# Queries and keys of a diffusion layer, computed with channels on partitions and read back in four parts

## The chip, the core and the metric

The kernel runs on one core of a Trainium2 chip. The metric is the time of one execution in microseconds (us) of the device; the profile's span leaves out a little at its ends. The engines are TensorE (PE in the profile, with its weight loads as PEld), VectorE (DVE), ScalarE (ACT), GpSimd (POOL) and SyncE (SP), which issues most transfers.

## What is computed

One layer of a diffusion backbone: 1024 latent tokens of 1024 channels and 256 context tokens are normalised and modulated, run through differential attention and a bidirectional state-space mixer side by side, merged, and then through a mixture of 64 experts. The part that the change touches is the first projection, the rotary embedding of queries and keys, and what the attention reads of them:

```python
q, k, v, z, xbc, dt_raw, gates = jnp.split(h @ w_in, IN_SPLITS, axis=-1)
...
q = apply_rope(q.reshape(nb, ns, N_ATTN_HEADS, 2, ATTN_DH), cos, sin)
k = apply_rope(k.reshape(nb, ns, N_ATTN_HEADS, 2, ATTN_DH), cos, sin)
...
kc = (hc @ w_k).reshape(nb, nl, N_ATTN_HEADS, 2, ATTN_DH)
...
k_all = jnp.concatenate([kc, k], axis=1)
...
def apply_rope(u, cos, sin):
    half = ATTN_DH // 2
    uf = u.astype(jnp.float32)
    rot = jnp.concatenate([-uf[..., half:], uf[..., :half]], axis=-1)
    return (uf * cos[:, None, None, :] + rot * sin[:, None, None, :]).astype(u.dtype)
```

There are 8 heads of two halves (c = 0, 1), each half with 64 channels of q and k. Context tokens have keys but no rotation and no queries.

## The kernel before

The kernel goes through its stages one behind the other, each one's end mixed with the next one's start: normalisation and q, k, v (0 to 391 us), the state-space mixer (to about 1040), attention (to about 1500), the branches and their merge (to about 1640), the experts (to the end).

**What sets the order.** The instructions are emitted by a planner at build time, the class `Flow`. Each piece of work is a Python generator, a stream with a priority, that yields what it needs next (a tile, a free buffer of a ring, an engine). The planner has a clock of its own for each engine and costs for each operation (a GpSimd transfer is put at 1050 ns of that engine), and always goes on with the stream that can start first; at a tie, the higher priority. So a change of one stream's operations can move the instructions of all others, and every engine then runs its own queue strictly in that order.

**Precision.** Every product is made in three matmuls (`mm3`, L420): numbers are split in a high and a low part (`hi`, `lo` for weights, `hh`, `hl` for h), and high x high, high x low and low x high are summed in a PSUM bank. The split is a cast by ScalarE (`F.acopy`, L165) and a subtraction by VectorE (`F.tt`, L172). `F.ptt` (L176) is the GpSimd form.

**q, k and v (`norm_and_qkv`, L492).** Six blocks of 512 columns of the weights, k, v, q, k, v, q, with 8 chunks of 128 channels each. `weights` loads and splits a block's weights, `modulate` makes h of the three groups of tokens (g = 0: the 256 of the context; g = 1, 2: 512 latent tokens each; h lies with channels on partitions) from transposes of x. `main` runs over tiles of 128 tokens: the tile's h is the stationary side, 512 columns of weights stream, and 24 matmuls fill one bank of the ring `acc` (4 banks). In the first block, the first three tiles are done in two halves of the channels (k 0 to 3, then 4 to 7). The adaLN vectors (`wa`, `cw`, `adab`, `wacc`) are worked out meanwhile.

**After a tile (`post_qk`, L662).** The bank has 128 tokens on partitions. VectorE multiplies it with the rope table (one product `ra` of 512 columns, two `rb` of 256), GpSimd adds the two into `r` (L176; for context tokens ScalarE copies instead), TensorE transposes `r` in four pieces into a bank of `tr` (L153), ScalarE casts this to the high part `sa`, VectorE subtracts for the low part `sb`. Two tiles share an `sa` and an `sb`; when both are full, SyncE stores them to DRAM (`s.qk`) in parts of 64 partitions.

**The seam.** `mixer_t` (L791) starts with dt: matmuls with 64 columns of weights, a fold (`aux<-fold,G`), then ScalarE and VectorE work out dt (`dtn`), which TensorE reads as `aux<-dtn,cst`. The convolution's matmuls (`acc<-hh,hi` with 128 columns) come beside these.

**Attention.** A tile `qk` of 128 partitions x 3328 numbers holds all that a head's half needs: for q its high and low part, for k its high and low part, so 1.70 MB. `attention_ahead` (L1326) loads them with `swdma` (L225), issued from GpSimd's queue, into a ring of three buffers: one transfer for each (h, c), when a buffer comes free. The scores are the matmuls `sps<-qk`; `e` is VectorE's and ScalarE's softmax, `tr<-cst,e` transposes it and `pv<-wr,vv` is the product with v. `branches` (L1196) gives matmuls of the merge (`bacc`, three for each product) as work of lower priority that fills gaps of TensorE in the planner's clock.

Of the kernel before, what the change touches and what calls it, by code (L numbers as in the profile page):

```python
# [9 lines left out]
F32 = mybir.dt.float32  # L10
F32R = mybir.dt.float32r
# [3 lines left out]
ALU = mybir.AluOpType  # L15
# [4 lines left out]
P = 128  # L20
D = 1024
KC = 8
T = 1024
# [26 lines left out]
def host_consts():  # L50
    j = np.arange(P)
    eye = np.eye(P, dtype=np.float32)
    le = (j[:, None] <= j[None, :]).astype(np.float32)
    ge = (j[:, None] >= j[None, :]).astype(np.float32)
    ones = np.ones((P, P), np.float32)
    cst = np.concatenate([eye, le, ge, ones], axis=1)
    row = np.repeat(np.arange(T // 64, dtype=np.float32), 64)
    col = np.tile(np.arange(64, dtype=np.float32), T // 64)
    inv = np.float32(10000.0) ** (-np.arange(0, 32, 2, dtype=np.float32) / np.float32(32))
    inv = inv.astype(np.float32)  # L60
    ang = np.concatenate([row[:, None] * inv, col[:, None] * inv], axis=-1)
    cos, sin = np.cos(ang), np.sin(ang)
    rope = np.concatenate([cos, cos, -sin, sin], axis=-1).astype(np.float32)
# [313 lines left out]
class Layer:  # L377
# [114 lines left out]
    def norm_and_qkv(s):  # L492
# [28 lines left out]
        st = {"wa": [], "x": 0, "w": 0, "normed": 0, "mod": 0, "done": [set(), set(), set()], "cols": 0, "blocks": 0, "ada": False, "q": None, "two": {}}  # L521
# [114 lines left out]

        def weights():
            for n, (kind, j) in enumerate(blocks):
                c0 = {"q": COL_Q, "k": COL_K, "v": COL_V}[kind] + j * 512
                for a in (0, 4):  # L640
# [8 lines left out]
                    yield from s.splits([(hi[:, b:b + 2], lo[:, b:b + 2], raw[:, b:b + 2]) for b in (0, 2)],  # L649
# [12 lines left out]
        def post_qk(ps, kind, j, t):  # L662
            yield [lambda: st["q"] is not None]
            rr, ras, rbs, sas, sbs, rope = (st["q"][n] for n in ("r", "ra", "rb", "sa", "sb", "rope"))
            if t < 2:
                yield [ps, rr, "ACT"]
                r = rr.get()
                F.acopy(r, ps.rearrange("p (h x) -> p h x", x=64))
                acc.put(ps)
            else:  # L670
                yield [ps, rope, ras, rbs, "DVE"]
                cs = rope[:, t - 2, :]
                pv = ps.rearrange("p (h x) -> p h x", x=64)
                ra, rb = ras.get(), rbs.get()
# [3 lines left out]
                acc.put(ps)  # L678
                yield [ra, rb, rr, "POOL"]
                r = rr.get()  # L680
                F.ptt(r, ra, rb, ALU.add)
                ras.put(ra)
                rbs.put(rb)
            yield [r, tr]
# [3 lines left out]
            two = st["two"].setdefault((kind, j, t // 2), [])  # L688
            yield [pt, "ACT"] + ([] if two else [sas, sbs])
            if not two:  # L690
                two += [sas.get(), sbs.get(), 0]
            a, b = two[:2]
            (av, bv), pv = (w.rearrange("p (m h c) -> h p m c", m=4, h=2)[t % 2] for w in (a, b)), pt.rearrange("p (m c) -> p m c", m=4)
            F.acopy(av, pv)
            yield [a, "DVE"]
            F.tt(bv, pv, av.bitcast(F32), ALU.subtract)
            tr.put(pt)
            two[2] += 1
            if two[2] == 2:
                o0 = (t // 2 - (kind == "q")) * 2 * P  # L700
                dst = s.qk[j].rearrange("(m u) (v x) c -> v u x m c", u=2, v=2)
                for w, v, o in ((a, 0, 0), (a, 1, 0), (b, 0, T), (b, 1, T)) if kind == "q" else ((a, 0, 2 * T), (b, 1, 2 * T)):
                    for u in range(2):
                        F.dma(dst[v, u][:, :, o + o0:o + o0 + 2 * P], w[64 * u:64 * u + 64].bitcast(F32).rearrange("x (m c) -> x m c", m=4))
                sas.put(a)
                sbs.put(b)
            rr.put(r)

        def main():
            for n, (kind, j) in enumerate(blocks):  # L710
                tiles = list(range(2 if kind == "q" else 0, 10))
                steps = [(t, 0, KC) for t in tiles]
                if n == 0:
                    steps = [(t, a, a + 4) for a in (0, 4) for t in tiles[:NH]] + steps[NH:]
                banks = {}
                for t, k0, k1 in steps:
                    yield [lambda: len(ready) >= 2 * n + k1 // 4]
                    tok = slice(t * P, (t + 1) * P)
                    g = 0 if t < 2 else 1 if t < 6 else 2
                    sl = slice((t - spans[g][0]) * P, (t - spans[g][0] + 1) * P)  # L720
                    hh, hl = s.h[g]
                    yield [lambda: st["done"][g].issuperset(range(k0, k1))] + ([] if k0 else [acc])
                    ps = banks.pop(t) if k0 else acc.get()
                    for k in range(k0, k1):
                        wh, wl = ready[2 * n + k // 4]
                        if k % 4 == 0:
                            yield [wh, wl, hh, hl]
                        s.mm3(ps, hh[:, k, sl], hl[:, k, sl], wh[:, k % 4], wl[:, k % 4], k == 0, k == KC - 1)
                    if k1 < KC:
                        banks[t] = ps  # L730
                    else:
                        F.spawn(1, post_v(ps, j, tok) if kind == "v" else post_qk(ps, kind, j, t))
                ws = ready[2 * n:2 * n + 2]
                his, los = sets[n % 2]
                for hi, lo in ws:
# [14 lines left out]
        st["q"] = q = {"r": s.ring(qp, [P, 8, 64], "r", 2), "ra": s.ring(qp, [P, 8, 64], "ra", 2),  # L750
                       "rb": s.ring(qp, [P, 8, 64], "rb", 2), "sa": s.ring(qp, [P, 1024], "sa", 2, F32R),
                       "sb": s.ring(qp, [P, 1024], "sb", 2, F32R), "rope": qp.tile([P, 8, P], F32, name="rope")}
        F.dma(q["rope"], I["rope"].rearrange("(t p) c -> p t c", p=P))
# [572 lines left out]
    def attention_ahead(s, go):  # L1326

        F = s.F
# [1172 lines left out]
```

## Time and profile before

| | |
|---|---|
| timed runs, median (lowest to highest) | 2770.72 us (2765.67 to 2773.66), 3 runs |
| the profiled execution | 2762.38 us, span 2760.1 us |
| TensorE busy | 2610.2 us, 95% of the span |
| VectorE, ScalarE, GpSimd busy | 73%, 49%, 33% |
| granted TensorE clock, mean | 0.979 |

The profile is of one execution. In the timeline the end of a matmul is modelled and runs over into the next one, so what a matmul costs is read from the distance of two starts, not from its duration. [...] Idle time before an instruction stands in brackets with what ended it.

### The profile page before, as it was taken

The numbers are of one execution on the slowest core, as the hardware profiler recorded it, in microseconds if no ns is written. First come the engines' busy times: TensorE is split into PE (matmuls) and PEld (weight loads), VectorE is DVE, ScalarE is ACT, GpSimd is POOL, SyncE is SP. The second block draws the span as 40 slices with busy tenths as digits, with TensorE's granted clock in tenths as the row PEclk, the third lists the DMA queues.
The fourth block names the chain that finished last, engine by engine and source line by source line (L and its number), as shares of the span: only waits on it lengthen the run. The fifth ranks groups of instructions, "written<-read, shape, count | busy, mean of one in ns | idle before, by whom it ended". The sixth has DMA issues, their size and how long they took to land.

```text
span 2760.1 us, 41127 instructions
## 1 busy us (share of the span) xinstructions
PE 2610.2 (95%) x14561; PEld 2099.0 (76%) x14561; DVE 2012.4 (73%) x4680; ACT 1341.9 (49%) x2104; POOL 920.9 (33%) x669
## 2 busy tenths in 40 slices
PE   7999999999999998999999999899999999999992
PEld 4888878878787776888888778677787787777771
DVE  6878133777776657888896657877879898888864
ACT  4211113344444446666675432335566666666652
POOL 0111010445354531000000000044667766777761
PEclk9999999999999999999999999999999999999996
DMA  7767253242425345322422872468999999999998
GB/s 275 226 205 220 62 149 102 69 145 77 138 77 149 91 120 186 119 86 87 142 97 75 263 252 107 168 234 288 292 319 315 339 333 311 315 314 307 296 308 251
DMA packets 275409, 545.67 MB, mean 198 GB/s; under 512 B 31562, under 2 KB 166835, under 8 KB 248194
## 3 DMA queue, kind: packets, MB, share of 16 engines
q1 hardware_dynamic: 238178, 432.95, 46.0%
q0 software_dynamic: 35872, 105.88, 14.7%
q10 hardware_dynamic: 1152, 4.19, 0.4%
q8 instruction: 115, 1.88, 0.3%
q14 instruction: 92, 0.75, 0.1%
HBM read 433.78 MB, written 124.73 MB: 202 GB/s over the span
## 4 chain that ended last, share of the span: by engine, by line
PE 63%; DMA 8%; DVE 8%; issue 3%; POOL 2%; ACT 2%; SPq 0%; ACTq 0%; POOLq 0%; DVEq 0%
PE gu L149 18%; PE acc L149 11%; PE dn L149 9%; PE bacc L149 6%; PE sps L149 5%; PE pv L149 4%; PE xt L153 3%; DMA cr<-cumd,crow 2%; PE tr L153 2%; PE aux L149 2%; DVE G L188 2%; DMA qk<-qk 2%; PE py L149 1%; DVE W L181 1%; PE hT L153 1%
## 5 line engine op out<-in xcount | busy, mean ns | idle before, releaser
L149 PE MATMUL acc<-hh,hi 128*128 128x512 f32 (+2 forms) x760 | 304.8, 401 | 1.3 <-DVE ux L188 1.3
L172 DVE TENSOR_TENSOR gl<-raw,gh 128x1024 fp32r<-128x1024 f32 x240 | 288.7, 1218 | 19.7 <-ACT gh L165 19.4
L149 PE MATMUL acc<-hl,hi 128*128 128x512 f32 (+2 forms) x760 | 289.5, 381 | 0.0
L149 PE MATMUL acc<-hh,lo 128*128 128x512 f32 (+1 forms) x736 | 281.0, 382 | 3.0 <-DVE lo L172 3.0
L149 PE MATMUL gu<-gh,xh 128*128 128x512 f32 (+3 forms) x672 | 279.5, 416 | 0.0
L149 PE MATMUL gu<-gh,xl 128*128 128x512 f32 (+3 forms) x672 | 264.6, 394 | 0.0
L149 PE MATMUL gu<-gl,xh 128*128 128x512 f32 (+3 forms) x672 | 264.3, 393 | 0.2 <-DVE gl L172 0.2
L165 ACT CAST gh<-raw 128x1024 fp32r<-128x1024 f32 x240 | 246.0, 1052 | 30.6 <-PE gu L149 21.2
L263 POOL DMA_INDIRECT cr<-cumd,crow x98 | 134.1, 1368 | 319.0 <-DMA wtab<-sc 282.5
L194 DVE TENSOR_SCALAR_CACHE_REDUCE e<-sps 128x512 f32<-128x512 f32 (+1 forms) x384 | 214.4, 597 | 33.9 <-PE sps L149 33.6
L269 POOL DMA_INDIRECT yacc<-y,tk x98 | 189.4, 1933 | 80.8 <-DMA yacc<-y,tk 14.4
L149 PE MATMUL sps<-qk 128*128 128x512 f32 (+1 forms) x768 | 196.1, 387 | 11.2 <-DMA qk<-qk 6.1
L157 ACT ACTIVATE e<-e,st 128x1280 f32<-128x1280 f32 x128 | 174.8, 1366 | 31.8 <-DVE st L203 31.6
L263 POOL DMA_INDIRECT wc<-wtab,tk x98 | 153.8, 1570 | 86.5 <-DVE tk L183 58.3
L149 PE MATMUL acc<-hi,hh 128*128 128x512 f32 x448 | 182.0, 406 | 0.0
L149 PE MATMUL acc<-hi,hl 128*128 128x512 f32 x448 | 176.6, 394 | 0.4 <-DVE hl L172 0.4
L149 PE MATMUL acc<-lo,hh 128*128 128x512 f32 x448 | 176.6, 394 | 0.0
L149 PEld LDWEIGHTS sps<-qk 128*128 128x128 f32 x768 | 141.4, 192 | 43.9 <-DVE e L194 9.8
L149 PEld LDWEIGHTS acc<-hh,hi 128*128 128x128 f32 (+1 forms) x760 | 142.5, 187 | 32.7 <-issue 4.2
L149 PE MATMUL pv<-wr,vv 128*128 128x256 f32 x640 | 164.6, 380 | 0.0
L149 PEld LDWEIGHTS acc<-hh,lo 128*128 128x128 f32 x736 | 138.8, 189 | 32.9 <-DVE lo L172 4.0
L149 PEld LDWEIGHTS acc<-hl,hi 128*128 128x128 f32 (+1 forms) x760 | 142.6, 188 | 27.4 <-issue 0.8
(327 smaller groups left out, 6246.5 us busy)
## 6 DMA issues: line engine op xcount, KB each, us to landing
raw<-in_w_e_gate_dram SPq DMA_DIRECT2D x64, 1024.0 KB, 9.2
raw<-in_w_e_up_dram SPq DMA_DIRECT2D x64, 1024.0 KB, 11.4
draw<-in_w_e_down_dram SPq DMA_DIRECT2D x64, 1024.0 KB, 9.9
qk<-qk POOLq DMA_DIRECT2D x16, 1664.0 KB, 10.4
raw<-in_w_in_dram SPq DMA_DIRECT2D x40, 512.0 KB, 4.7
wada<-in_w_ada_dram SPq DMA_DIRECT2D x32, 512.0 KB, 5.6
R<-acd SPq DMA_DIRECT2D x64, 256.0 KB, 5.4
qk<-sa SPq DMA_DIRECT2D x52, 256.0 KB, 4.1
```

What stands on the lines that cost most here:

```text
L149: s.nc.tensor.matmul(out, l, r, start=start, stop=stop)
L153: s.nc.tensor.transpose(out, in_, ident)
L157: s.nc.scalar.activation(out, in_, fn, **kw)
L165: s.nc.scalar.copy(out, in_)
L172: s.nc.vector.tensor_tensor(out, a, b, op=op)
L181: s.nc.vector.tensor_scalar(out, a, s1, s2, op0=op0)
L188: s.nc.vector.scalar_tensor_tensor(out, a, sc, b, op0=op0, op1=op1)
L194: s.nc.vector.tensor_scalar(out, a, s1, None, op0=op0, op1=op1, accum_out=acc)
L263: s.nc.gpsimd.indirect_dma_start(out=out, out_offset=None, in_=table, in_offset=bass.IndirectOffsetOnAxis(ap=idx, axis=0), **kw)
L269: s.nc.gpsimd.indirect_dma_start(out=table, out_offset=bass.IndirectOffsetOnAxis(ap=idx, axis=0), in_=in_, in_offset=None, compute_op=ALU. ...
```

## The change

The weights of q and k become the stationary side and h streams, so a bank holds 128 channels x 512 tokens (256 for the context) with channels on partitions. `weights` writes the split weights in another order of columns (`byhalf`): the first 32 channels of every half-head in one set of 128 columns, the other 32 in another, so that the two numbers of a rotary pair lie on the same partition of two banks. A unit is (g, r, f): token group, which 128 of the pairs, and which of the two (f). `post_qk` works on a pair of units: four VectorE products with the cos and sin tables (now laid out with channels on partitions and 1024 tokens along the row), a subtraction and an addition by GpSimd, two casts and two subtractions for the low parts, and stores of 128 partitions. The transposes of `r`, and the tiles `r` and `ra`, are gone. A half of a head then lies in four places of 32 rows in DRAM, and four GpSimd transfers of 32 partitions each read it; each asks for GpSimd anew. In the first block the units start with g = 1.

```diff
-        def post_qk(ps, kind, j, t):
+        def post_qk(pair, kind, j, g, r):
...
-                F.tt(ra, pv, cs[:, None, 0:64].to_broadcast([P, 8, 64]), ALU.mult)
-                F.tt(rb[:, :, 0:32], pv[:, :, 32:64], cs[:, None, 64:96].to_broadcast([P, 8, 32]), ALU.mult)
-                F.tt(rb[:, :, 32:64], pv[:, :, 0:32], cs[:, None, 96:128].to_broadcast([P, 8, 32]), ALU.mult)
...
-                F.ptt(r, ra, rb, ALU.add)
...
+                F.tt(l[0], pair[0], cos, ALU.mult)
+                F.tt(rb[:, 1], pair[0], sin, ALU.mult)
+                acc.put(pair[0])
+                yield [pair[1], "DVE"]
+                F.tt(rb[:, 0], pair[1], sin, ALU.mult)
+                F.tt(l[1], pair[1], cos, ALU.mult)
+                acc.put(pair[1])
+                yield [rb, "POOL"]
+                F.ptt(l[0], l[0], rb[:, 0], ALU.subtract)
+                yield [rb, "POOL"]
+                F.ptt(l[1], l[1], rb[:, 1], ALU.add)
...
-            pt = tr.get()
-            for m in range(4):
-                F.tp(pt[:, m * P:(m + 1) * P], r[:, 2 * m:2 * m + 2].rearrange("p u x -> p (u x)"), s.ident)
...
+            for f in range(2):
+                yield [src[f], "ACT"]
+                F.acopy(hi[:, f * 512:f * 512 + n], src[f])
+            for f in range(2):
+                yield [hi, "DVE"]
+                F.tt(l[f], src[f], hi[:, f * 512:f * 512 + n].bitcast(F32), ALU.subtract)
...
-                steps = [(t, 0, KC) for t in tiles]
+                    units = [(g, r, f) for g in ((0, 1, 2) if kind == "k" else (1, 2)) for r in range(2) for f in range(2)]
+                    if n == 0:
+                        units = units[4:6] + units[:4] + units[6:]
...
-                        s.mm3(ps, hh[:, k, sl], hl[:, k, sl], wh[:, k % 4], wl[:, k % 4], k == 0, k == KC - 1)
...
+                            a, b = (byhalf(w)[:, u[2], k % 4, u[1] * P:(u[1] + 1) * P] for w in (wh, wl))
+                            s.mm3(ps[:, :spans[g][1] * P], a, b, hh[:, k], hl[:, k], k == 0, k == KC - 1)
...
-                    F.swdma(t, s.qk[h // 4][2 * (h % 4) + c])
+                    for x in range(4):
+                        yield ["POOL"]
+                        F.swdma(t[32 * x:32 * x + 32], s.qk[h // 4].rearrange("(r x) (y i) c -> r y x i c", x=4, y=4)[h % 4 // 2, h % 2 * 2 + c, x])
```

**TensorE at the start of the first block.** Before, behind the transposes of x of the context tokens (`tr`) and adaLN matmuls (`acc<-wa,cw`), with hi_172, lo_173 the first weights and hh_81, hl_82 the context's h:

```order
L153 MATMUL tr<-cst,x_88 128x128
L149 MATMUL acc<-wa,cw 32x512 x4
L149 MATMUL acc<-hi_172,hh_81 128x512
L149 MATMUL acc<-lo_173,hh_81 128x512
L149 MATMUL acc<-hi_172,hl_82 128x512
```

The change at the same place:

```order
L153 MATMUL tr<-cst,x_88 128x128
L149 MATMUL acc<-wa,cw 32x512 x8
L149 MATMUL adab<-fold,row 128x2 x4
L153 MATMUL tr<-cst,x_89 128x128
L153 MATMUL tr<-cst,x_90 128x128
```

The 24 matmuls on the context's h (12 of them begin here, 12 more behind the next `acc<-wa,cw`) are not there any more; the transposes of the latent tokens' x (x_89 on) follow at once.

**TensorE at the seam with the mixer.** Before, from the last dt matmul (`acc<-hl_82,hi`) on:

```order
L149 MATMUL acc<-hl_82,hi 64x256
L149 MATMUL aux<-fold,G 128x32 x10
L149 MATMUL acc<-hh_83,hi 128x512
L149 MATMUL acc<-hl_84,hi 128x512
L149 MATMUL acc<-hh_83,lo 128x512
```

The change there:

```order
L149 MATMUL acc<-hl_82,hi 64x256
L149 MATMUL aux<-fold,G 128x32 x10
L149 MATMUL aux<-dtn,cst 128x160 x2
L149 MATMUL aux<-dtn,cst 128x320
L149 MATMUL aux<-cst,dtn 16x128 x4
L149 MATMUL acc<-hh_83,hi 128x512
L149 MATMUL acc<-hl_84,hi 128x512
L149 MATMUL acc<-hh_83,lo 128x512
```

Before, nine convolution matmuls stand between the fold and the first `aux<-dtn,cst` (three of them are shown); now the uses of dt follow the fold at once and the convolution comes behind them.

**TensorE ahead of the first use of a loaded half-head**, the head change with the third of the seven new halves that are awaited (qk_10170 before, qk_10085 in the change). Before:

```order
L153 MATMUL tr_10235<-cst_107,e_9924 128x128
L153 MATMUL tr_10235<-cst_107,e_9994 128x128
L149 MATMUL pv_10167<-wr_10186,vv_9630 128x256 x2
L149 MATMUL sps_10247<-qk_10170 128x512 x2
L149 MATMUL sps_10251<-qk_10170 128x512 x2
```

The change:

```order
L149 MATMUL bacc_10186<-bxh_8451,bwl_10029 128x512
L149 MATMUL bacc_10186<-bxh_8466,bwh_10028 128x512
L149 MATMUL bacc_10186<-bxl_8467,bwh_10028 128x512
L149 MATMUL bacc_10186<-bxh_8466,bwl_10029 128x512
L149 MATMUL sps_10216<-qk_10085 128x512 x2
L149 MATMUL sps_10219<-qk_10085 128x512 x2
```

Before, transposes and products with v stand right ahead of the scores; now the last of 30 branch matmuls do, which stand between the product with v and the scores.

**GpSimd, the first loads.** Before:

```order
L228 DMA qk<-qk_62 128x3328 x3
L228 DMA vv<-vv_64 128x10x128
L176 TENSOR_TENSOR bwl<-braw,bwh 128x512
L228 DMA qk<-qk_62 128x3328
L228 DMA vv<-vv_64 128x10x128
L228 DMA qk<-qk_62 128x3328 x2
```

The change:

```order
L228 DMA qk<-qk_62 32x3328 x12
L228 DMA vv<-vv_64 128x10x128
L176 TENSOR_TENSOR bwl<-braw,bwh 128x512 x2
L228 DMA qk<-qk_62 32x3328 x4
L228 DMA vv<-vv_64 128x10x128
L228 DMA qk<-qk_62 32x3328 x8
```

Each load of a half-head has become four, in the same places.

## Rows read from the trace of the kernel before

**Rows 1.** Windows: span; PE, PEld, DVE, ACT, POOL busy (count), PEclk, DMA, GB/s.

```profile
50.00:100.00 50.00, 48.22 (x249) 39.62 (x249) 44.19 (x101) 20.45 (x31) 8.15 (x5) 1.00 0.51 151
100.00:150.00 50.00, 50.00 (x232) 40.66 (x231) 39.33 (x94) 9.18 (x13) 4.70 (x3) 1.00 0.75 228
350.00:355.00 5.00, 5.00 (x19) 4.02 (x19) 0.69 (x1) 0.59 (x1) 1.06 (x1) 0.66 0.10 29
390.00:400.00 10.00, 9.24 (x36) 5.39 (x37) 0.69 (x1) 2.68 (x4) 0.71 (x1) 0.83 0.63 166
1060.00:1095.00 35.00, 29.39 (x131) 22.29 (x132) 34.15 (x103) 23.21 (x37) 1.30 (x1) 0.90 0.19 58
```

**Rows 2.** TensorE timeline, one transpose group: start, duration, operation.

```profile
84.45 0.39 PE L149 MATMUL acc<-hi,hl 128*128 128x512 f32 x1
84.68 0.60 PE L153 MATMUL tr<-cst,r 128*128 128x128 f32 x4
85.03 0.48 PE L149 MATMUL acc<-hi,hh 128*128 128x512 f32 x1
```

**Rows 3.** The tile tr: TensorE's transposes of r, duration min/median/max, first and last.

```profile
L153 PE MATMUL tr<-cst,r x144: 270/272/330, 59.2 to 391.1; 128*128 128x128 f32 x144
```

**Rows 4.** TensorE timeline in the mixer: 256-column matmuls behind each other.

```profile
423.00 0.28 PE L149 MATMUL acc<-hl,hi 128*128 128x256 f32 x1
423.12 0.28 PE L149 MATMUL acc<-hh,lo 128*128 128x256 f32 x1
```

**Rows 5.** TensorE timeline at 350 us; in brackets the idle time before.

```profile
349.86 0.71 PE L153 MATMUL tr<-cst,r 128*128 128x128 f32 x4 [2.30 <-POOL r L176]
```

**Rows 6.** TensorE timeline at the start of the first block.

```profile
31.94 0.80 PE L149 MATMUL acc<-hi,hh 128*128 128x512 f32 x1
...
38.93 0.40 PE L149 MATMUL acc<-hi,hl 128*128 128x512 f32 x1
...
47.68 0.48 PE L149 MATMUL acc<-hi,hh 128*128 128x512 f32 x1
```

**Rows 7.** TensorE timeline at the seam with the mixer.

```profile
390.76 0.66 PE L153 MATMUL tr<-cst,r 128*128 128x128 f32 x4 [2.51 <-POOL r L176]
...
402.20 2.42 PE L149 MATMUL aux<-fold,G 64*128 64x32 f32 x20
...
409.10 0.54 PE L149 MATMUL aux<-dtn,cst 128*128 128x160 f32 x2 [0.25 <-DVE dtn L188]
```

**Rows 8.** VectorE groups by form, 20 to 392 us: busy, mean ns | idle before.

```profile
L172 DVE TENSOR_TENSOR rb<-acc,rope 128x256 f32<-128x256 f32 x64 | 23.9, 414 | 0.0
L172 DVE TENSOR_TENSOR ra<-acc,rope 128x512 f32<-128x512 f32 x32 | 22.0, 688 | 28.1 <-PE acc L149 26.3 <-PE adab L153 1.7
...
L172 DVE TENSOR_TENSOR hl<-hf,hh 128x512 fp32r<-128x512 f32 x16 | 12.4, 778 | 0.3
```

**Rows 9.** GpSimd groups, 20 to 392 us.

```profile
L176 POOL TENSOR_TENSOR r<-ra,rb 128x512 f32<-128x512 f32 x32 | 44.6, 1395 | 345.6 <-DVE rb L172 341.3 <-DMA qk<-sb 4.3
```

**Rows 10.** The tile qk, 1040 to 1500 us: GpSimd's issues (ns), and landings.

```profile
L228 POOL DMA_DIRECT2D qk<-qk x16: 531/542/728, 1041.5 to 1419.5; - x16
...
DMA to landing us min/median/max: 7.3/10.4/18.3
```

**Rows 11.** Chain of waits, the second head change: start, duration.

```profile
1149.06 8.00 DMA qk<-qk
```

**Rows 12.** TensorE timeline, first matmuls on newly loaded halves.

```profile
1157.19 1.41 PE L149 MATMUL sps<-qk 128*128 128x512 f32 x6 [0.89 <-DMA qk<-qk]
...
1213.62 2.22 PE L149 MATMUL sps<-qk 128*128 128x512 f32 x6 [3.31 <-DMA qk<-qk]
```

**Rows 13.** TensorE's waits, 1040 to 1500 us: us in total, times, longest.

```profile
PE sps L149 <- DMA qk<-qk: 6.1, 6, 3.3
```

**Rows 14.** Windows with q stores (64 partitions), then a load of qk (128).

```profile
394.00:398.00 4.00, 4.00 (x17) 2.24 (x17) 0.00 (x0) 0.58 (x1) 0.00 (x0) 0.91 0.99 262
1152.00:1155.00 3.00, 3.00 (x20) 2.66 (x19) 2.96 (x12) 1.94 (x3) 0.54 (x1) 1.00 1.07 408
```

More of the change, by code (lines that the diff above doesn't have):

```diff
@@ L62, in host_consts @@
     cos, sin = np.cos(ang), np.sin(ang)
-    rope = np.concatenate([cos, cos, -sin, sin], axis=-1).astype(np.float32)
+    rope = np.stack([np.tile(q.T, (4, 1)) for q in (cos, sin)], axis=1).astype(np.float32)
     e = np.arange(64)
@@ L648, in weights @@
                     hi, lo = his.get(), los.get()
-                    yield from s.splits([(hi[:, b:b + 2], lo[:, b:b + 2], raw[:, b:b + 2]) for b in (0, 2)],
+                    parts = [[w[:, b:b + 2] for w in (hi, lo, raw)] for b in (0, 2)]
+                    if kind != "v":
+                        parts = [[byhalf(w)[:, :, b:b + 2].rearrange("p f k (y i) -> p f (k y) i", i=32) for w in (hi, lo)] +
+                                 [raw[:, b:b + 2].rearrange("p k (y f i) -> p f (k y) i", f=2, i=32)] for b in (0, 2)]
+                    yield from s.splits(parts,
                                         lambda raw=raw, w=(hi, lo): (raws.put(raw), ready.append(w)), 1)
@@ new lines, in post_qk @@
+            rbs, sas, sbs, rope = (st["q"][n] for n in ("rb", "sa", "sb", "rope"))
+            n = spans[g][1] * P
+            yield [sbs, pair[0]]
+            lo = sbs.get(F32)
+            l = [lo[:, f * 512:f * 512 + n] for f in range(2)]
+            if g:
+                cos, sin = (rope[:, i, (g - 1) * 512:g * 512] for i in range(2))
+                yield [pair[0], rope, rbs, "DVE"]
+                rb = rbs.get()
+                F.tt(l[0], pair[0], cos, ALU.mult)
[9 more added lines that the diff above has]
+                F.ptt(l[1], l[1], rb[:, 1], ALU.add)
+                rbs.put(rb)
@@ new lines, in post_qk @@
+            src = l if g else [b[:, :n] for b in pair]
+            yield [sas]
+            hi = sas.get()
+            for f in range(2):
[4 more added lines that the diff above has]
+                F.tt(l[f], src[f], hi[:, f * 512:f * 512 + n].bitcast(F32), ALU.subtract)
+            if g == 0:
+                acc.put(*pair)
+            o0 = (spans[g][0] - 2 * (kind == "q")) * P
@@ L709, in main @@
+            dst = s.qk[j].rearrange("(r v f) p c -> r v f p c", v=2, f=2)
+            for f in range(2):
+                for w, v, o in ((hi, 0, 0), (hi, 1, 0), (lo, 0, T), (lo, 1, T)) if kind == "q" else ((hi, 0, 2 * T), (lo, 1, 2 * T)):
+                    F.dma(dst[r, v, f][:, o + o0:o + o0 + n], (w[:, f * 512:f * 512 + n].bitcast(F32) if w is hi else l[f]))
+            sas.put(hi)
+            sbs.put(lo)
         def main():
             for n, (kind, j) in enumerate(blocks):
-                tiles = list(range(2 if kind == "q" else 0, 10))
@@ L712, in main @@
-                steps = [(t, 0, KC) for t in tiles]
+                if kind == "v":
+                    units = [(0 if t < 2 else 1 if t < 6 else 2, t) for t in range(10)]
+                else:
+                    units = [(g, r, f) for g in ((0, 1, 2) if kind == "k" else (1, 2)) for r in range(2) for f in range(2)]
+                    if n == 0:
+                        units = units[4:6] + units[:4] + units[6:]
+                steps = [(u, 0, KC) for u in units]
                 if n == 0:
-                    steps = [(t, a, a + 4) for a in (0, 4) for t in tiles[:NH]] + steps[NH:]
@@ L721, in main @@
                     hh, hl = s.h[g]
                     yield [lambda: st["done"][g].issuperset(range(k0, k1))] + ([] if k0 else [acc])
-                    ps = banks.pop(t) if k0 else acc.get()
+                    ps = banks.pop(u) if k0 else acc.get()
                     for k in range(k0, k1):
```

70 lines of the change are left out of this document (22 added, 48 removed).

## The prediction

> **What bounds the kernel now.** I read the page's busy shares first, which the table above repeats: TensorE is busy for 95% of the span, so the question for every stage is whether TensorE works less or waits less. The windows of the query, key and value stage, which ends at 391 us, say that there are no gaps while its data is there: TensorE 50.00 us of 50 from 100 to 150, VectorE 39.33, and the DMA engines at 0.75; from 50 to 100 it is 48.22, with VectorE at 44.19 [rows 1]. Only the first 48 us are bound by transfers. So from there to 391 us a TensorE instruction taken out is time taken out, and the work of VectorE, ScalarE and GpSimd counts only where it comes so late that TensorE waits. Then I read the timeline of TensorE around the transposes, at the start and at the seam with the mixer, and last the loads of the attention and who waits for them.
>
> **1. The transposes go: -15.8 us.** A 512-column matmul takes a slot of 0.23 us (84.45 to 84.68). A group of four transposes holds the queue from 84.68 to 85.03, 0.35 us, and the first matmul behind it is longer than its neighbour by 0.09 (0.48 after 0.39), so a group costs 0.44 us [rows 2]. There are 144 transposes of r, 36 groups [rows 3]: 36 x 0.44 = 15.8 us. The matmuls that make q and k stay: weights and h change sides, each unit of 512 tokens streams 24 x 512 columns, and a context unit 24 x 256. Narrow ones could have taken more than half a slot, since a weight load comes with each, but in the mixer 256-column matmuls with full weights follow each other at 0.12 us (423.00 to 423.12) [rows 4]. So nothing is added here.
>
> **2. A wait for GpSimd goes: -4.0 us.** At 347 us TensorE waits 2.30 us for r, the sum that GpSimd makes ahead of the transposes [rows 5]. [...] What is late next there is an accumulator bank (part 5).
>
> **3. The start: +6.5 us.** Before, the first two key tiles are those of the context, whose h is ready first, and 24 of their matmuls run between 31.94 and 39.16 us, in the stretch bound by transfers; the next matmul for q and k starts at 47.68 [rows 6]. In the changed order these 24 are gone from there, and the block begins with latent tokens at the place of 47.68. Nothing else fills the hole, so 24 x 0.234 = 5.6 us of work moves into the dense part. Twenty-four transposes of x then stand in a row in front of the second half of the channels, and VectorE, which casts and splits what they give, has little room there (44.19 of 50) [rows 1]: 0 to 3 us more. I take 1. Bounds 4 (the first latent matmuls come a little earlier, since 24 no longer stand ahead of them) to 9.
>
> **4. The seam with the mixer: -1 us.** The last transposes wait 2.51 us for r [rows 7], and the clock is 0.83 from 390 to 400, 1.7 us [rows 1]: 4.2 us go, as in part 2. But before, nine convolution matmuls stand between the fold of dt (402.20, 2.42 long) and its use at 409.10, and fill the 4.5 us in which ScalarE and VectorE work out dt [rows 7]. In the new order the uses of dt come first and TensorE waits. The nine, which took those 4.5 us, then follow at the full slot, 9 x 0.234 = 2.1 us, so the loss is about 2.1, and up to 1.5 more if the clock falls after such a wait as it did at 350. The sum is -2 to +1.6; I take -1.
>
> **5. VectorE, ScalarE, GpSimd and SyncE: +1 us.** For rope VectorE spent 32 x 0.688 (ra) + 64 x 0.414 (rb) = 48.5 us; it now has 64 products of 512 columns, 64 x 0.688 = 44.0 us. The 36 lower parts, one input of which lay in PSUM, now mostly have both in SBUF; the nearest row is the lower part of h, 0.778, against 0.688 for ra, which reads PSUM [rows 8]: 36 x 0.09 = +3.2 us. So VectorE has the same work. The weights are now cast and split through a permutation in runs of 32 numbers; rb reads such runs already, at 0.414 for 256 columns against 0.688 for 512 plain ones, so I cost it at nothing. GpSimd has the same 32 sums at 1.4 us [rows 9]. A pair now holds two of the four accumulator banks until VectorE has read them (4 x 0.69 = 2.8 us after the second is full), while the other two take 11.2 us to fill, so 8 us of TensorE's work cover it; the cover is gone if VectorE's queue is 8 us late. SyncE issues 112 stores instead of 104. Bounds 0 to 5; I take 1, since VectorE is nowhere full.
>
> **6. Attention: -1 us.** A head's half is loaded by one GpSimd transfer when its buffer comes free; it lands after 7.3 us at best and 10.4 in the middle [rows 10]. The steady case: released and issued at 1149.06, landed 8.00 later, and TensorE had waited 0.89 us at 1157.19; so TensorE wants the data 7.24 us after the release [rows 11, 12]. All such waits sum to 6.1 us, the longest 3.3 [rows 13]. The change has four transfers of 32 partitions. Each costs GpSimd 0.54 us to issue [rows 10], so the last quarter leaves 1.6 us later, which the transfer of the first three hides. The transfer itself: 1.70 MB at 408 GB/s, seen in a 128-partition load, is 4.2 us; the 64-partition stores ran at 262 GB/s with the DMA engines at 0.99 [rows 14], which makes 6.5; if halving once more cost the same factor, 168 GB/s and 10.1 us. So the landing takes between 7.5 and 14.5 us. I take 10, near the row of the stores, since four transfers in flight touch all partitions as a single one does. Against that the planner now sets branch matmuls (bacc) in front of the first use: 0, 30, 30, 21, 12, 6 and 24 of them at seven head changes, where it had none but for 15 at the last. At 0.234 us each TensorE wants the data 7.2, 14.3, 14.3, 12.2, 10.0, 8.6 and 12.9 us after the release. With a landing of 10 us the waits are 2.8 + 1.4 = 4.2 instead of 6.1: -2. The ramp (1060 to 1095: TensorE 29.39 of 35, VectorE 34.15) [rows 1] takes in some 30 such matmuls, worth up to -6, but its first load may land up to 5 us later; I take -1. The branch stage behind the attention, from which these matmuls are taken, has 2 us of waits uncovered: +2. Bounds of the sum -6 to +9.
>
> [...]
>
> **Sum.** -15.8 - 4.0 + 6.5 - 1 + 1 - 1 = -14.3 us. The MoE behind is bound by its transfers, but they start where the program reaches it, so the gain stays. The profiled execution was 2762.4 us with a span of 2760.1, below all three timed runs (2765.7 to 2773.7), so I apply the difference to their median: 2770.7 - 14.3 = 2756.4 us. Against its own execution it would be 2748.
>
> **Rivals.** *The quarters are slow and every head change pays (slower).* With 14.5 us to land, the waits are 7.3 + 0.2 + 0.2 + 2.3 + 4.5 + 5.9 + 1.6 = 22 us instead of 6.1: +16. Four are long enough for a lowered clock behind them, as at 1213.62, where six matmuls took 2.22 us against 1.41 at 1157.19 [rows 12], 1.3 us each: +5. The first load of the ramp +5. In place of my -1 that is +26: -13.3 + 26 = +13, 2783 us. From a landing of 10.7 us on the waits pass those of before; the whole change turns into a loss near 13. For it speaks the rate of the 64-partition stores, against it the filler. *The start and the seam eat the gain (no change).* Start +9, seam +1.6, late pairs +4, attention +4: -15.8 - 4 + 18.6 = -1, 2769 us. For it speaks that 24 free matmuls are lost for certain and that VectorE has 6 us of 50 free there. *The ramp takes all the filler (faster still).* Attention -6, start +4, seam -2, nothing in part 5: -24, 2747 us. *VectorE becomes the bound of the stage.* If each lower part stood still for one of GpSimd's sums, 32 x 1.4 = 45 us over 340 is 6.6 in 50: 46 of 50 from 100 on, still not full, but above 50 before 100; +5 there, 2761 us.
>
> [...]
>
> **How the numbers follow.** Chances: forecast 0.48, slow quarters 0.14, gain eaten 0.18, ramp filled 0.12, VectorE the bound 0.08. A measurement of this kernel can tell 0.3%, 8.3 us, from no change: faster is under 2762.4, slower above 2779. Nine tenths of the forecast are faster, all of the filled ramp and half of VectorE's case: 0.58. Slower: most of the slow quarters and a tail of the others, 0.16. Same: 0.26. The range takes in the filled ramp, the bounds of the forecast's unknown costs and the eaten gain, and leaves out most of the slow quarters: 2746 to 2778.
>
> **What would show it.** Right: no transposes of r; TensorE 50 of 50 us from 100 to 385 with no wait at 347; first q and k matmul near 47; the mixer's dt matmuls from 375 to 381 instead of 391.2; landings of qk near 10 us and waits for them of 3 to 8 us in all. Wrong: landings of 13 us and more with waits of over 15 in the attention; waits of TensorE on an accumulator that VectorE holds in the q and k blocks; a mixer that starts at 387 or later.

## The result, and the profile after

The changed kernel is slower: 2786.0 us in the middle of seven runs (2782.5 to 2795.4) against 2768.5 of seven runs before (2765.7 to 2773.7). The ratio is 1.0068, with a 95% interval from 1.0052 to 1.0084. The forecast was 2756 us and faster, with a range of 2746 to 2778, so it was wrong in sign and in range.

The page of the changed kernel shows TensorE busy as long as before (2610.6 us against 2610.2), although the 144 transposes are gone, and a span 24 us longer than in [rows 1]'s execution:

```profile
span 2784.3 us, 41079 instructions
...
PE 2610.6 (94%) x14513; PEld 2099.0 (75%) x14513; DVE 2010.1 (72%) x4651; ACT 1340.5 (48%) x2104; POOL 941.6 (34%) x718
...
qk<-qk POOLq DMA_DIRECT2D x64, 416.0 KB
```

The first step is to find the stage. I took four marks from the rows of single tiles: the first matmul of the mixer's dt, the first and the last branch matmul (`bacc`), and the last product of the experts (`dn`). The third column is a second profile of the kernel before (experiment "before_again"), the last the best version found.

| us | before | before_again | after | one_load_spread |
|---|---|---|---|---|
| first dt matmul of the mixer | 391.2 | 394.0 | 372.7 | 372.8 |
| first branch matmul | 1035.1 | 1031.9 | 1017.4 | 1016.6 |
| last branch matmul | 1638.4 | 1632.8 | 1650.3 | 1615.3 |
| last product of the experts | 2699.3 | 2707.8 | 2724.2 | 2688.3 |

So the new q, k and v stage gains 18 to 21 us, and at the first branch matmul 14 to 18 of them are still there. Between the first and the last branch matmul, which is the attention with its ramp and its end, the changed kernel takes 632.9 us against 603.3 and 600.9. About 30 us are lost there. The windows between these two marks, first of the changed kernel, then of the first profile before (columns as in [rows 1]), say of what kind the loss is:

```profile
1017.40:1650.30 632.90, 591.10 (x3054) 498.27 (x3055) 479.56 (x1377) 361.34 (x594) 44.70 (x76) 0.96 0.52 138
```

```profile
1035.10:1638.40 603.30, 581.50 (x3054) 491.27 (x3055) 478.99 (x1378) 361.66 (x594) 20.79 (x27) 0.99 0.43 145
```

TensorE runs the same 3054 matmuls. It stands idle for 41.8 us instead of 21.8, so 20 us are waits; it is busy for 591.1 instead of 581.5, so 10 us are work at a lower granted clock (PEclk, as a share of full speed), 0.96 against 0.99.

**The q, k and v stage.** Two rows of the changed kernel's timeline of TensorE and one window (columns as in [rows 1]) say that it went as hoped. They answer to [rows 1, 5, 7]:

```profile
372.72 0.40 PE L149 MATMUL acc<-hh,hi 128*64 128x512 f32 x1
...
388.99 2.75 PE L149 MATMUL aux<-dtn,cst 128*128 128x160 f32 x6 [4.47 <-DVE dtn L188]
```

```profile
100.00:372.00 272.00, 272.00 (x1259) 224.82 (x1258) 163.75 (x341) 45.15 (x68) 35.03 (x26) 1.00 0.57 187
```

TensorE has no gap from 100 to 372 us; the waits for r are gone; and the new wait for dt at the seam, 4.47 us, is where part 4 put it. What the clock does behind it stands under point 4 below.

**The ramp of the attention.** The waits of TensorE from 1040 to 1510 us, which answer to [rows 13]:

```profile
PE bacc L149 <- ACT bwh L165: 12.2, 2, 7.3
PE tr L153 <- ACT wr L165: 7.9, 6, 3.5
PE sps L149 <- DMA qk<-qk: 6.1, 3, 3.8
PE sps L149 <- DVE e L194: 5.3, 4, 2.9
```

The waits for qk are 6.1 us, to the digit what they were. One wait is new, 12.2 us for the high part of branch weights (`bwh`, a cast by ScalarE), and one has grown from 0.7 us in both profiles of before to 7.9, that for ScalarE's copies of the transposed softmax (`wr`). The timeline of TensorE at the ramp shows the first:

```profile
1037.72 1.40 PE L149 MATMUL sps<-qk 128*128 128x512 f32 x6
1046.40 0.80 PE L149 MATMUL bacc<-bxh,bwh 128*128 128x512 f32 x1 [7.28 <-ACT bwh L165]
1046.99 0.63 PE L149 MATMUL bacc<-bxl,bwh 128*128 128x512 f32 x1
1047.42 0.63 PE L149 MATMUL bacc<-bxh,bwl 128*128 128x512 f32 x1
...
1058.27 0.80 PE L149 MATMUL bacc<-bxh,bwh 128*128 128x512 f32 x1 [4.90 <-ACT bwh L165]
```

Behind the first scores stand branch matmuls whose weights are not there. TensorE waits 7.28 us, and the matmuls behind are 0.43 us apart instead of 0.23; behind the next scores it waits another 4.90. The chain of waits shows the load that the second wait is for, and the windows say why it is late:

```profile
1027.73 29.79 DMA braw<-in_w_branch_ssd_dram
```

```profile
1030.00:1040.00 10.00, 8.97 (x40) 6.99 (x38) 0.00 (x0) 0.60 (x1) 1.96 (x4) 1.00 1.15 227
1040.00:1050.00 10.00, 3.60 (x9) 2.79 (x10) 2.41 (x8) 3.04 (x3) 1.01 (x1) 0.56 1.19 241
...
1101.00:1104.00 3.00, 3.00 (x18) 2.66 (x18) 2.73 (x12) 2.30 (x4) 1.94 (x4) 1.00 1.13 226
```

A load of branch weights issued at 1027.73 lands 29.79 us later. In this time the DMA engines are full (1.15 and 1.19) and yet move only 227 and 241 GB/s; the first twelve quarters, 5.1 MB, are under way. At a head change (1101 to 1104) it is 226 GB/s, where the load of a whole half-head ran at 408 [rows 14].

**The head changes.** Of the wait that has grown, the waits of ScalarE give the cause. The first fence is the changed kernel from 1040 to 1510 us, the second the second profile of the kernel before from 1030 to 1480:

```profile
ACT bwh L165 <- DMA braw<-in_w_branch_ssd_dram: 36.2, 6, 14.9
```

```profile
ACT bwh L165 <- DMA braw<-in_w_branch_ssd_dram: 0.5, 2, 0.3
```

The branch work pulled forward brings its casts with it. Of the 36.2 us some 22 are at the ramp and 14 at the head changes, where a softmax copy can stand right behind the cast that waits. The longest case, in the timelines of ScalarE and of TensorE:

```profile
1243.53 0.62 ACT L165 CAST bwh<-braw 128x512 fp32r<-128x512 f32 x1 [6.18 <-DMA braw<-in_w_branch_ssd_dram]
1244.05 0.58 ACT L165 COPY wr<-tr 128x512 f32<-128x512 f32 x1
```

```profile
1244.68 0.66 PE L153 MATMUL tr<-cst,e 128*128 128x128 f32 x4 [3.51 <-ACT wr L165]
```

ScalarE waits 6.18 us for branch weights, runs the cast and then the copy, and TensorE's next transposes, which wait for the copy, come 3.51 us late.

### The profile page after: what moved, and what is told of

The parts are those of the page before. It is cut to its first block, busy times and chain, and to the rows that moved or that the text cites. A ratio compares the mean times of both kernels' runs of the same rounds, so it can differ in the third digit from the quotient of the medians.

```text
span 2784.3 us, 41079 instructions
## 1 busy us (share of the span) xinstructions
PE 2610.6 (94%) x14513; PEld 2099.0 (75%) x14513; DVE 2010.1 (72%) x4651; ACT 1340.5 (48%) x2104; POOL 941.6 (34%) x718
## 4 chain that ended last, share of the span: by engine, by line
PE 76%; DMA 8%; DVE 8%; issue 3%; ACT 2%; POOL 2%; SPq 1%; ACTq 0%; POOLq 0%; DVEq 0%
PE acc L149 21%; PE gu L149 20%; PE dn L149 10%; PE bacc L149 5%; PE sps L149 4%; PE pv L149 4%; PE xt L153 3%; PE tr L153 2%; PE aux L149 2%; DMA braw<-in_w_branch_ssd_dram 2%; DVE G L188 2%; DMA cr<-cumd,crow 1%; DMA ysg<-braw 1%; PE hT L153 1%; POOL W L176 1%
## 5 line engine op out<-in xcount | busy, mean ns | idle before, releaser
L149 PE MATMUL acc<-hh,hi 128*128 128x512 f32 (+3 forms) x1080 | 424.3, 393 | 1.3 <-DVE ux L188 1.3
L149 PE MATMUL acc<-hl,hi 128*128 128x512 f32 (+3 forms) x1080 | 406.9, 377 | 0.0
L149 PE MATMUL acc<-hh,lo 128*128 128x512 f32 (+1 forms) x1056 | 399.5, 378 | 2.3 <-DVE lo L172 2.3
L149 PEld LDWEIGHTS acc<-hh,hi 128*128 128x128 f32 (+1 forms) x1080 | 202.4, 187 | 42.5 <-issue 3.4
L149 PEld LDWEIGHTS acc<-hh,lo 128*128 128x128 f32 x1056 | 199.0, 188 | 42.4 <-DVE lo L172 2.7
L149 PEld LDWEIGHTS acc<-hl,hi 128*128 128x128 f32 (+1 forms) x1080 | 202.6, 188 | 37.2
L263 POOL DMA_INDIRECT xg<-htab,tk x98 | 134.4, 1372 | 89.7 <-PE hT L153 51.7
L176 POOL TENSOR_TENSOR sb<-sb,rb 128x512 f32<-128x512 f32 x32 | 42.8, 1360 | 332.9 <-DVE rb L172 332.9
L165 ACT COPY wr<-tr 128x512 f32<-128x512 f32 x160 | 93.1, 582 | 127.4 <-PE tr L153 126.9
```

The lines of the kernel that those rows point to most:

```text
L149: s.nc.tensor.matmul(out, l, r, start=start, stop=stop)
L165: s.nc.scalar.copy(out, in_)
L176: s.nc.gpsimd.tensor_tensor(out, a, b, op=op)
L263: s.nc.gpsimd.indirect_dma_start(out=out, out_offset=None, in_=table, in_offset=bass.IndirectOffsetOnAxis(ap=idx, axis=0), **kw)
```

## The experiments

Two causes can make this picture. *Rate*: transfers to 32 neighbouring partitions run at about half the rate of one to 128 (226 to 241 GB/s against 408) and hold up the transfers that are issued while they run (29.79 us for a load of branch weights). *Order*: the planner, told of four slow loads, sets branch matmuls ahead of their data. Both came with the same edit. The kernels below separate them; most differ only in how the loop over `(h, c)` loads a half-head and in what the planner is told of it.

**The reading alone: before_with_quarters.** The kernel before, with

```diff
-                    F.swdma(t, s.qk[h // 4][2 * (h % 4) + c])
+                    src = s.qk[h // 4][2 * (h % 4) + c]
+                    for x in range(4):
+                        yield ["POOL"]
+                        F.swdma(t[32 * x:32 * x + 32], src[32 * x:32 * x + 32])
```

> The kernel before with nothing changed but the loads: four transfers of 32 partitions each, and the planner told of four. If the reading is the whole loss and the q, k, v stage a gain of about 14 us, this is the slowest of all: 2768 + 18 + 14, so 2795 to 2805 us. If the loss needs the new stage (its order at the seam), it is no slower than the changed kernel, 2786 us or less.

It took 2806.4 us, 1.0142 of before (1.0120 to 1.0163): +38 us, just above the 2795 to 2805 expected. The planner was told of four here, so this is transfers and order together. The reading alone costs more than the whole change, and the new stage gives back about 20 us of it (2806 to 2786). That the loss needs the new order at the seam falls away.

**A detour: one_load, quarters_order_of_one and one_load_order_of_quarters.** To read a half-head with one transfer, I first made it contiguous in DRAM, so that the stores of 128 partitions scatter into four places:

```diff
-            dst = s.qk[j].rearrange("(r v f) p c -> r v f p c", v=2, f=2)
+            dst = s.qk[j].rearrange("(r y) (v f i) c -> r v f y i c", y=4, v=2, f=2)
...
-                    for x in range(4):
-                        yield ["POOL"]
-                        F.swdma(t[32 * x:32 * x + 32], s.qk[h // 4].rearrange("(r x) (y i) c -> r y x i c", x=4, y=4)[h % 4 // 2, h % 2 * 2 + c, x])
+                    F.swdma(t, s.qk[h // 4][2 * (h % 4) + c])
```

> The changed kernel, but q and k are stored so that a half-head is contiguous, and one GpSimd transfer of 128 partitions loads it, as before; the planner is told of one, and sets the branch matmuls as it did before (0 of them ahead of the first use at six head changes, 15 at the last). If the loss comes from reading in quarters, by whichever way, this keeps the gain of the q, k, v stage: mixer at about 373 us (391 before), a seam that gives some 5 us back, about 14 us faster than before, 2750 to 2758 us. If the loss lay in the new layout itself or in the experts' stage, it would be near 2768 or above.

It took 2845.4 us, 1.0277 of before, far from both values expected. The stores themselves had become slow. VectorE's waits from 50 to 400 us, and a window in which TensorE starves:

```profile
DVE sb L172 <- DMA qk<-sb: 38.2, 5, 19.8
```

```profile
235.00:245.00 10.00, 2.62 (x12) 2.62 (x13) 4.12 (x13) 2.06 (x3) 0.00 (x0) 0.52 0.40 136
```

The DMA engines are not full (0.40, where the changed kernel has 1.04 from 235 to 245 us), and still VectorE waits up to 19.8 us for a buffer that a store holds; in the changed kernel all such waits sum to 2.3 us. The store's DRAM side now begins with a dimension of 4; whether that is what slows it is not shown, since no run varied the size. As a test of the reads, this kernel and the two beside it are clouded by these stores; their differences are still of use.

> As one_load, with the same order of instructions on TensorE, but four real transfers of 32 partitions in place of each load, and the planner still told of one. Theory of the rate (quarters run at half rate and hold back what is queued behind them): landings of 10 to 11 us, 3 us of wait at each of seven head changes in place of 0.9, branch weights late at the ramp; 15 to 25 us slower than one_load. Theory of the order (only the branch matmuls set ahead of their data cost): no more than 8 us slower than one_load.

2883.1 us: with the same order of instructions, quarters cost 37.7 us more than one load, where 15 to 25 were expected. TensorE's waits for qk grew from 4.5 to 26.3 us.

> The order of the changed kernel on TensorE (0, 30, 30, 21, 12, 6, 24 branch matmuls ahead of the first use, 12 behind the first scores), since the planner is told of four loads, but one real transfer of 128 partitions. Theory of the order: TensorE still waits for the branch weights at the ramp, most of 12 us, and ScalarE's casts hold back the attention; about as slow as the changed kernel, 2778 to 2788 us. Theory of the rate: the branch weights land in time, and the time is near one_load, 2750 to 2762 us.

2849.7 us: the order alone costs 4.4 us. So rate, by both; but on a base whose stores were slow, which I wanted to be rid of.

**One load with the plain stores: one_load_spread.** The stores stay as the change has them. The sum over the 128 partitions of `qk` does not mind which row lies on which partition, as long as q and k agree, so one transfer can take row i of quarter x to partition 4i + x:

```diff
-                    for x in range(4):
-                        yield ["POOL"]
-                        F.swdma(t[32 * x:32 * x + 32], s.qk[h // 4].rearrange("(r x) (y i) c -> r y x i c", x=4, y=4)[h % 4 // 2, h % 2 * 2 + c, x])
+                    F.swdma(t, s.qk[h // 4].rearrange("(r x) (y i) c -> r y i x c", x=4, y=4)[h % 4 // 2, h % 2 * 2 + c])
```

> The changed kernel with its stores as they are, but each half-head read by one GpSimd transfer of 128 partitions, row i of quarter x landing on partition 4i + x; the sum over partitions does not mind the order. The planner is told of one, and sets the branch matmuls as before. If the quarters' loads are the loss, all of it goes and the gain of the new stage is left: 2786 less about 38 (what quarters cost the kernel before), so 2745 to 2755 us, waits for qk of 4 to 8 us. If the order of rows makes the load slow too, waits of 20 us and more and 2775 or above.

2746.8 us, 0.9924 of before (0.9903 to 0.9944): the largest gain of all, 39 us under the changed kernel. Its waits for qk are 2.8 us, and in the ramp the engines move 387 GB/s:

```profile
PE sps L149 <- DMA qk<-qk: 2.8, 4, 1.5
```

```profile
1030.00:1040.00 10.00, 9.94 (x45) 7.81 (x45) 2.67 (x10) 2.11 (x2) 0.00 (x0) 1.00 1.02 387
```

**Four transfers, other partitions: quarters_spread.** The changed kernel with its four transfers, its order and its stores, and one slice altered:

```diff
-                        F.swdma(t[32 * x:32 * x + 32], s.qk[h // 4].rearrange("(r x) (y i) c -> r y x i c", x=4, y=4)[h % 4 // 2, h % 2 * 2 + c, x])
+                        F.swdma(t[x::4], s.qk[h // 4].rearrange("(r x) (y i) c -> r y x i c", x=4, y=4)[h % 4 // 2, h % 2 * 2 + c, x])
```

> The changed kernel with its order, its four transfers for each half-head and what the planner is told, but each transfer lands on every fourth partition (x, 4 + x, 8 + x, ...) instead of 32 neighbours. If what is slow is 32 neighbouring partitions, the DMA engines pass 350 GB/s and more while they are read, the branch weights land in time and the time is 2750 to 2765 us. If what costs is the number of transfers, their size or the branch matmuls set ahead, it is as slow as the changed kernel, 2780 to 2790.

2758.9 us, 0.9957 of before (0.9944 to 0.9969), 27 us under the changed kernel. Same bytes, same number of transfers, same order on TensorE; only the partitions of each quarter differ. The window of the ramp and the wait for the branch weights:

```profile
1030.00:1040.00 10.00, 10.00 (x46) 8.30 (x46) 2.92 (x9) 2.73 (x4) 2.58 (x4) 1.00 1.02 390
```

```profile
PE bacc L149 <- ACT bwh L165: 3.4, 1, 3.4
```

390 GB/s instead of 227, and 3.4 us of wait instead of 12.2. The load of branch weights that landed after 29.79 us there, issued at 1027.73, takes 18.04 here:

```profile
1027.40 18.04 DMA braw<-in_w_branch_ssd_dram
```

This is the cleanest of the tests: that the quarters go to 32 neighbouring partitions is the cause of these 27 us, since number, size and order of the transfers are the same in both. What their number costs, the table below bounds.

**The two causes crossed.** Four more kernels, on the change's plain stores, complete the table. Where the planner is told of one load, `swdma` issues the transfers but counts the cost once, and the branch matmuls stand where they stood before; where it is told of four with one real load, the other way round. The edit for the first of them (the others differ in the slice only):

```diff
+                    for x in range(4):
+                        F.swdma(t[32 * x:32 * x + 32], s.qk[h // 4].rearrange("(r x) (y i) c -> r y x i c", x=4, y=4)[h % 4 // 2, h % 2 * 2 + c, x], (t, s.qk[h // 4].rearrange("(r x) (y i) c -> r y i x c", x=4, y=4)[h % 4 // 2, h % 2 * 2 + c]) if x == 3 else None)
...
+        if cost is None:
+            return
```

> The changed kernel with its plain stores and its four transfers of 32 neighbouring partitions, but the planner told of one load, so that no branch matmul stands ahead of the first use of a half-head at six head changes. If the rate of these transfers is the cause and the order only moves it about, the waits for qk grow to 20 us and more (landings of 10.5, wanted after 7.2, seven times, and the first one) and the time is 2775 to 2790 us. If the branch matmuls set ahead were the cause, it is within 10 us of one_load_spread, under 2757 us.

> As neighbours_order_of_one, but two transfers of 64 neighbouring partitions each. If the rate falls in proportion to the partitions of one transfer, 64 is faster than 32 and the loss about half of that of neighbours_order_of_one. If 64 neighbours are as slow as 32, as the stores of the kernel before at 262 GB/s let one suspect, the loss is nearly the same, within 8 us.

> As neighbours_order_of_one, but each of the four transfers lands on every fourth partition. Against one_load_spread only the number of transfers differs, against neighbours_order_of_one only the partitions. If the partitions are the cause, 2745 to 2757 us; if four transfers in place of one cost by themselves, 2765 or above.

> One transfer of 128 partitions for each half-head, as in one_load_spread, in the order of the changed kernel, since the planner is told of four. Rate: the branch weights land in time, and the time is 2746 to 2758 us; what it is above one_load_spread (2747) is the price of the order alone, 4 us by one_load_order_of_quarters against one_load. Order: 2775 or above.

The medians in us, before being 2768 to 2771:

| how a half-head is loaded | planner told of one | planner told of four |
|---|---|---|
| four transfers of 32 neighbours | 2790.5 | 2786.0 (the change) |
| two transfers of 64 neighbours | 2788.3 | |
| four transfers, every fourth partition | 2756.7 | 2758.9 |
| one transfer of 128 | 2746.8 | 2758.4 |

Down a column the rate costs 27 to 44 us. Along a row the order costs nothing that can be told with four slow loads (1.0063 of its before, 1.0040 to 1.0086, against 1.0068 of the change), 2 us with four spread ones, and 12 with a single one, more than the 4 us of the detour. With slow loads and the old order the same loss stands elsewhere. TensorE's waits in neighbours_order_of_one, from 1000 to 1520 us, and its window of the ramp:

```profile
PE sps L149 <- DMA qk<-qk: 27.7, 8, 6.7
```

```profile
1040.00:1050.00 10.00, 3.31 (x10) 2.74 (x10) 3.05 (x14) 1.45 (x2) 1.01 (x1) 0.56 1.14 251
```

27.7 us of waits for qk here, 6.1 + 12.2 + 7.9 = 26.2 us of three kinds in the changed kernel. And two halves of 64 neighbours are as slow as four quarters, 242 GB/s at a full 1.18:

```profile
1030.00:1040.00 10.00, 6.33 (x28) 4.80 (x26) 1.81 (x7) 1.46 (x2) 0.00 (x0) 0.94 1.18 242
```

Why 32 and 64 neighbours run alike, and every fourth partition at 390 GB/s, no run shows. That four spread transfers stay 10 us behind one (2756.7 against 2746.8) is not explained; their waits for qk are 6.9 us against 2.8, which is less than half of it. So the number of transfers, at the same partitions, costs up to 10 us.

**The start: one_load_context_first.** As one_load_spread, without the line that puts latent units first:

```diff
-                    if n == 0:
-                        units = units[4:6] + units[:4] + units[6:]
```

> As one_load_spread, but the first block's units begin with those of the context, so that 36 matmuls of 256 columns stand in the stretch that is bound by transfers, in place of none. By part 3 of the prediction the matmuls lost from the start cost 5.6 us and the row of transposes 1; 36 x 0.117 = 4.2 us come back: 3 to 6 us faster than one_load_spread at its mixer and at the end. If the start does not set the end, no difference.

Its mixer starts at 370.1 us instead of 372.8, so 2.7 us came back, a little under the 3 to 6 expected. The time, 2748.0 us (0.9931, 0.9918 to 0.9945), can't be told from one_load_spread's. At the mixer the start counts, but for less than I put on it; whether the 2.7 us reach the end, these times do not show.

**Chance in the experts: before_again.**

> The kernel before, unchanged, for a second profile. In its first profile the experts' stage had no wait on the supply of instructions and took 947 us from its first transpose to its last product; in the changed kernel and in all four others it had 7 to 9 us of such waits and took 952 to 961. If that belongs to the program, this profile has none again; if it falls by chance, some 7 us of it may stand here and the span be near 2772.

One execution took 2770.9 us. The waits of TensorE from 1640 us on in this second profile, and behind it in the changed kernel's (`issue` is time in which TensorE waited for nothing that the profile shows, so that a lack of instructions, as I called it, is only a guess at their cause):

```profile
PE gu L149 <- issue: 7.2, 14, 1.1
```

```profile
PE gu L149 <- issue: 6.9, 16, 1.1
```

In the first profile of before, this wait was absent, and the experts took 947 us from the first transpose of their input to their last product, where they took 961 in the second. Every other kernel's profile shown here has 6 to 9 us of it. So the first profile of before is the odd one, and the wait is no part of the change: of the 24 us between the two first profiles some 13 are the experts' stage, half of them this wait, and the attention's loss less the stage's gain is the rest.

## Why the prediction was wrong, point by point

**1, the transposes, and 2, the wait for r: right.** The mixer starts 18.5 to 21.2 us earlier, ahead of the 375 to 381 us that I had named; parts 1 to 3, 5 and the wait of part 4 had given 15.8 + 4.0 + 2.5 - 6.5 - 1 = 14.8. The terms were not measured one by one. Of the 4.0 of part 2, 2.30 are the wait [rows 5] and 1.7 were put down to the granted clock of 0.66 behind it [rows 1]; no run shows these 1.7 us on their own. What the trace of before shows there is matmuls 0.42 to 0.43 us apart (350.80, 351.22, 351.65) instead of 0.234, and in the changed kernel the clock is 1.00 from 100 to 372 us. The 256-column matmuls with a weight load each follow each other at 0.12 us in the changed kernel too (65.78, 65.90, 66.02), as taken from [rows 4].

**3, the start: mechanism right, size too large.** The 24 matmuls are gone from the stretch of transfers, and the row of transposes stalls 1.27 us. Counted at 100 us, the changed kernel has 6 to 7 matmuls for q, k and v fewer behind it, while the kernel before had also done 28 transposes of r by then: 6.5 x 0.234 + 7 x 0.44 = 4.6 us, within the bounds of 4 to 9 but under the 6.5 taken. The experiment brought back 2.7 of them.

**4, the seam: the wait right, the clock not.** The wait for dt was 4.47 us where 4.5 was read from [rows 7]. But the clock, which I had only as a bound, did fall with it. Two windows of the changed kernel:

```profile
386.00:392.00 6.00, 3.01 (x8) 1.80 (x9) 2.23 (x5) 4.39 (x7) 0.00 (x0) 0.50 0.00 0
393.00:400.00 7.00, 7.00 (x37) 4.90 (x36) 3.46 (x7) 1.27 (x3) 0.00 (x0) 1.00 0.41 109
```

From 386 to 392, in the second half of the wait and in the work behind it, the granted clock is 0.50, and from 393 on 1.00. TensorE is busy for 3.0 of these 6 us, so by estimate from 0.50 x 3.0 the lowered clock costs 1.5 us. The 1.7 us of lowered clock at 390 that part 4 counted as gone have moved behind the new wait.

**5, the other engines: right.** VectorE's rope products took 43.0 us (44.0 was forecast), a lower part 0.766 us (0.778), and TensorE never waited for an accumulator. The 1 us taken for late pairs was not needed. This disposes of the rival in which VectorE becomes the bound. These are the rows of the changed kernel, 20 to 392 us, which answer to [rows 8]:

```profile
L172 DVE TENSOR_TENSOR sb<-sb,sa 128x512 f32<-128x512 f32 x32 | 23.8, 766 | 9.5 <-ACT sa L165 8.8
L172 DVE TENSOR_TENSOR sb<-acc,rope 128x512 f32<-128x512 f32 x32 | 21.8, 682 | 4.3 <-DMA qk<-sb 2.3 <-PE acc L149 2.0
L172 DVE TENSOR_TENSOR rb<-acc,rope 128x512 f32<-128x512 f32 x32 | 21.2, 683 | 17.7 <-PE acc L149 17.7
```

**6, the attention: wrong, -1 forecast and about +30 measured.** The odd thing is that its two numbers were near: a landing of 10 us against 10.5 seen at a head change (issued from 1097.63 on, landed at 1108.12), and waits for qk of 4.2 against 6.1. Three steps failed.

- *The filler was taken for ready work.* I counted how many branch matmuls stand ahead of a first use and added them to the window at 0.234 us each. They need weights that come through the same DMA engines and ScalarE's queue, and the sum had no term for either. At the ramp they were worth "up to -6" in the sum and cost 12.2 us of waits, and behind them half-rate matmuls (clock 0.56 from 1040 to 1050).
- *A slow transfer was priced only by who waits for it.* The first three half-heads are loaded at once: by estimate, 5.1 MB at some 230 GB/s take 22 us, at 390 they take 13. A load of weights issued while they ran landed after 29.79 us, and after 18.04 with the fast quarters. I allowed 5 us for that, as a bound, for the first scores alone.
- *The rate was scaled by the number of partitions.* From 408 and 262 I went on to 168 GB/s for 32 partitions. 32 neighbours run at 213 to 251 GB/s and 64 at 208 to 242. The landing that I took, 10 us, came out right by luck: this error stood against another one, that four transfers in flight together would touch all partitions and so be nearly as fast as one (227 GB/s against 408).

None of the signs of being wrong that I had named came: where TensorE waited for a half-head at a head change, its landing took about 10.6 us, and the waits for qk came to 6.1 in all. For the attention they looked only at the new loads' own data, and the loss was in other work.

Of the rivals, "the quarters are slow" named the cause, the sign and, at 2783 us, nearly the time; its price went through waits at the head changes, which is what neighbours_order_of_one shows (27.7 us) and the changed kernel does not. I gave it 0.14, because the filler spoke against it.

## What to carry to other kernels

Price a slow transfer by the time for which it fills the DMA engines (here by estimate 22 us for the first three half-heads), and look at the transfers issued meanwhile and at what stands behind their consumers in each engine's order, not only at who waits for its own data. Where a tile must be read in parts, give each part partitions from the whole range (390 GB/s here, against 227 for 32 neighbours); where the consumer sums over partitions, their order is free, and one transfer with a permuted source was best here (2746.8 us). Work that a planner pulls into a gap covers nothing unless its operands, too, are there at that time (12.2 us of waits for branch weights here).

## What was not expected of the hardware

- Four transfers of 416 KB to every fourth partition move 390 GB/s, to 32 neighbours 227, with the DMA engines full in both (1.02 and 1.15), and two of 64 neighbours 242 (1.18).
- The kernel whose stores have a DRAM side that begins with a dimension of 4 had its DMA engines at 0.40 while TensorE starved, and was 77 us slower than before, which was more than any reading cost. That this dimension is the reason was not tested.
- The waits of TensorE that the profile puts down to `issue` in the experts' stage, 7.2 us in the second profile of before, were missing in the first one, from which the prediction was read, and their cause is open; the span was 2769 us in the second and 2760 in the first.
